# Adaptive max pooling: one 1 MB run of the input per partition, 47.5 KB loads pooled by one instruction each, two stores

## The chip, the cores and the metric

The kernel runs on one core of a Trainium2 chip; nothing else runs on the chip. The metric is the device time of an execution in microseconds (us), medians of several runs. All runs quoted here are with a granted clock of 1.0. KB and MB in sizes of runs and pitches are powers of two (1 MB = 1,048,576 bytes); MB and GB/s in the lines of the profile are decimal.

## The reference

The input is 32 x 256 x 4096 fp32 (134.2 MB), the output 32 x 256 x 256 fp32 (8.4 MB). The length is a multiple of the output size, so every window has 16 elements and none overlap:

```python
for i in range(output_size):
    start = int(i * length / output_size)
    end = int((i + 1) * length / output_size)
    result[:, :, i] = np.max(x[:, :, start:end], axis=-1)
```

In memory this is a maximum over each 16 consecutive numbers of a flat array. How the array is dealt out to the 128 partitions is free, and that is what the change is about.

## The kernel before

There are 8192 rows of 16 KB. 63 x 128 of them are cut into three regions; in each region a partition owns 21 consecutive rows. A load takes three rows (48 KB) per partition into a ring of nine row slots, three instructions on VectorE pool them, and all stores are issued after the last load. The last 128 rows are a load and a store of their own.

```python
    RING = 9
    G = 21
    N_GROUPS = 3
    LOAD = 3
    CUT = 15
    ...
    xg = xf[0:main].rearrange("(g p r) (o w) -> g p r o w", p=P, r=G, w=W)
    og = of[0:main].rearrange("(g p r) m -> g p (r m)", p=P, r=G)
    ...
    for g in range(N_GROUPS):
        for r in range(0, G, LOAD):
            at = n_read % RING
            nc.sync.dma_start(
                out=ring[:, at : at + LOAD], in_=xg[g][:, r : r + LOAD]
            )
            for i in range(LOAD):
                pooled(outs[g][:, (r + i) * O : (r + i + 1) * O], ring[:, at + i])
            n_read += LOAD
    ...
    for g in range(N_GROUPS - 1):
        nc.sync.dma_start(out=og[g], in_=outs[g])
    for a, b in ((0, CUT), (CUT, G)):
        ...
    nc.scalar.dma_start(out=ol, in_=spare)
```

Neighbouring partitions start 21 x 16 KB = 336 KB apart in HBM. This distance is called the pitch below.

Of the kernel before, what the change touches and what calls it, by code (L numbers as in the profile page):

```python
# [1 line left out]

# [4 lines left out]


@with_exitstack
def kernel(  # L10
    ctx: ExitStack,
    tc: tile.TileContext,
    x: bass.AP,
    output_size: bass.AP,
    out: bass.AP,
):



    nc = tc.nc  # L20
    P = nc.NUM_PARTITIONS
    fp32 = mybir.dt.float32

    B, C, L = x.shape
    O = int(output_size)
    assert L % O == 0, (L, O)
    W = L // O
    xf = x.flatten_outer_dims()
    of = out.flatten_outer_dims()
    rows = xf.shape[0]  # L30
    assert rows == 64 * P

    RING = 9
    G = 21
    N_GROUPS = 3
    LOAD = 3
    CUT = 15

    pool = ctx.enter_context(tc.tile_pool(name="pool", bufs=1))
    ring = pool.tile([P, RING, O, W], fp32, tag="ring", name="ring")  # L40
    outs = [
        pool.tile([P, G * O], fp32, tag=f"out{i}", name=f"out{i}")
        for i in range(N_GROUPS)
    ]

    main = N_GROUPS * G * P
    xg = xf[0:main].rearrange("(g p r) (o w) -> g p r o w", p=P, r=G, w=W)
    og = of[0:main].rearrange("(g p r) m -> g p (r m)", p=P, r=G)
    xl = xf[main:rows].rearrange("p (o w) -> p o w", w=W)
    ol = of[main:rows]  # L50

    def pooled(dst, src):
        nc.vector.reduce_max(out=dst, in_=src, axis=mybir.AxisListType.X)  # L53

    n_read = 0
    for g in range(N_GROUPS):
        for r in range(0, G, LOAD):
            at = n_read % RING
            nc.sync.dma_start(  # L59
                out=ring[:, at : at + LOAD], in_=xg[g][:, r : r + LOAD]  # L60
            )
            for i in range(LOAD):
                pooled(outs[g][:, (r + i) * O : (r + i + 1) * O], ring[:, at + i])
            n_read += LOAD

    at = n_read % RING
    spare = ring[:, (at + LOAD) % RING].rearrange("p o w -> p (o w)")[:, 0:O]
    nc.sync.dma_start(out=ring[:, at], in_=xl)
    pooled(spare, ring[:, at])

    for g in range(N_GROUPS - 1):
        nc.sync.dma_start(out=og[g], in_=outs[g])
    for a, b in ((0, CUT), (CUT, G)):
        nc.sync.dma_start(
            out=og[N_GROUPS - 1][:, a * O : b * O],
            in_=outs[N_GROUPS - 1][:, a * O : b * O],
        )
    nc.scalar.dma_start(out=ol, in_=spare)


# [1 line left out]
_INS = ['x', 'output_size']  # L82
_OUTS = [((32, 256, 256), 'float32')]

_NUMBERS = {'output_size': 256}


# [26 lines left out]
```

## Time and profile before

| | before |
|---|---|
| time, median of 6 runs | 335.94 us (335.76 to 336.12) |
| span of the profiled run | 334.3 us |
| moved by DMA | 142.6 MB, 427 GB/s over the span |
| queue of the loads and stores, share of the 16 engines' span | 98.9% |
| VectorE busy | 278.8 us (83%) |
| spacing of two loads of 6.29 MB | 14.53 us |

These lines are from the page of the kernel before: busy time by engine, bandwidth in 40 equal slices of the span, and the main DMA queue (packets, MB, share).

```profile
span 334.3 us, 157 instructions
...
DVE 278.8 (83%) x64; POOL 0.2 (0%) x4
...
GB/s 371 382 465 453 400 465 394 453 459 394 465 394 453 459 394 465 394 453 459 394 465 394 453 459 394 465 394 448 459 400 459 400 447 459 400 459 388 437 426 297
...
q1 hardware_dynamic: 3744, 142.48, 98.9%
...
```

The queue is full nearly from end to end, with 98.9% of the 16 engines' span: the transfers are the limit. The next lines, from the timeline of the same run, say the same of VectorE: start, duration, what ran, and in brackets how long VectorE had been idle and what it waited for.

```profile
...
start us, us, engine line op out<-in xcount [idle before <-releaser]
...
18.44 13.07 DVE L53 TENSOR_REDUCE out<-ring 128x256 f32<-128x4096 f32 x3 [18.44 <-DMA ring<-in_x_dram]
32.94 13.07 DVE L53 TENSOR_REDUCE out<-ring 128x256 f32<-128x4096 f32 x3 [1.43 <-DMA ring<-in_x_dram]
47.48 13.07 DVE L53 TENSOR_REDUCE out<-ring 128x256 f32<-128x4096 f32 x3 [1.47 <-DMA ring<-in_x_dram]
62.01 13.07 DVE L53 TENSOR_REDUCE out<-ring 128x256 f32<-128x4096 f32 x3 [1.45 <-DMA ring<-in_x_dram]
...
```

Each group of three reductions takes 13.07 us and the next load lands 14.53 us after the last (32.94 - 18.44 is 14.50, 47.48 - 32.94 is 14.54), so VectorE idles 1.46 us per load. 6.29 MB in 14.53 us is 433 GB/s. The windows view gives the bandwidth in stretches of the run (window, its length, VectorE busy and count, POOL busy and count, clock, DMA share, GB/s). The first stretch is the start-up, which matters below.

```profile
...
core 0: us, DVE busy (x) POOL busy (x), PEclk, DMA share, GB/s
5.00:35.00 30.00, 15.13 (x4) 0.00 (x0) 1.00 0.98 426
40.00:160.00 120.00, 108.31 (x26) 0.00 (x0) 1.00 1.00 433
...
```

The packet records of the trace are very even (a packet is one entry of these records; the 21 loads of 48 KB runs left 2688 of 48 KB, one per partition and load). A packet of 48 KB most often takes 1815 ns, one of 21 KB 799 ns. These two fit bytes / 27.2 GB/s plus about 9 ns per packet; this is called the fit below (packets of 15 and 6 KB took 573 and 234 ns, where it gives 574 and 235, and packets of 4 bytes 9 ns). 128 such packets per load or store are eight for each of the 16 engines in the mean.

### The profile page before, as it was taken

To read this page: it belongs to the slowest core of one execution; us is meant where nothing else is said; L and a number is where in the kernel's file an instruction comes from. 1 tells how busy PE (TensorE), PEld (TensorE's weight loads), DVE (VectorE), ACT (ScalarE), POOL (GpSimd) and SP (SyncE) were. 2 spreads that over 40 slices of the span, in tenths; PEclk is the share of its full clock that TensorE was granted. 3 is DMA by queue.
4 is the path that set the end of the run, shared out by engine and by line. 5 is a ranking of instruction groups with operands and counts; after the bars stand their busy time and mean duration, and the time that the engine had idled before them with its cause. 6 is when DMAs were issued, how large, how long until landed. Compare 5 with 4: busy or idle time off the path is not lost.

```text
span 334.3 us, 157 instructions
## 1 busy us (share of the span) xinstructions
DVE 278.8 (83%) x64; POOL 0.2 (0%) x4
## 2 busy tenths in 40 slices
DVE  0078989898898989889898898989889898988990
POOL 0000000000000000000000000000000000000000
DMA  9899999999999999999999999999999999999997
GB/s 371 382 465 453 400 465 394 453 459 394 465 394 453 459 394 465 394 453 459 394 465 394 453 459 394 465 394 448 459 400 459 400 447 459 400 459 388 437 426 297
DMA packets 3889, 142.62 MB, mean 427 GB/s; under 512 B 432, under 2 KB 560, under 8 KB 688
## 3 DMA queue, kind: packets, MB, share of 16 engines
q1 hardware_dynamic: 3744, 142.48, 98.9%
q10 hardware_dynamic: 144, 0.13, 0.1%
q14 instruction: 1, 0.01, 0.0%
HBM read 134.22 MB, written 8.39 MB: 427 GB/s over the span
## 4 chain that ended last, share of the span: by engine, by line
DMA 68%; DVE 26%; DVEq 2%; SPq 0%; issue 0%
DMA ring<-in_x_dram 68%; DVE out L53 25%; DVEq L109 2%; DVE ring L53 1%; SPq L59 0%
## 5 line engine op out<-in xcount | busy, mean ns | idle before, releaser
L53 DVE TENSOR_REDUCE out<-ring 128x256 f32<-128x4096 f32 x63 | 274.5, 4412 | 47.6 <-DMA ring<-in_x_dram 47.6
L53 DVE TENSOR_REDUCE ring<-ring 128x256 f32<-128x4096 f32 x1 | 4.4, 4410 | 0.0
L95 POOL MEMSET const-bfloat16-1.0<- 128x1 bf16 x1 | 0.1, 101 | 0.0
L95 POOL MEMSET const-uint8-127<- 128x1 uint8 x1 | 0.1, 101 | 0.0
L95 POOL MEMSET const-float32-0.0<- 128x1 f32 x1 | 0.1, 98 | 0.2 <-issue 0.2
L95 POOL MEMSET const-float32-1.0<- 128x1 f32 x1 | 0.1, 98 | 0.0
## 6 DMA issues: line engine op xcount, KB each, us to landing
ring<-in_x_dram SPq DMA_DIRECT2D x21, 6144.0 KB, 30.5
out_dram<-out SPq DMA_DIRECT2D x2, 2688.0 KB, 38.4
ring<-in_x_dram SPq DMA_DIRECT2D x1, 2048.0 KB, 29.5
out_dram<-out SPq DMA_DIRECT2D x1, 1920.0 KB, 38.2
out_dram<-out SPq DMA_DIRECT2D x1, 768.0 KB, 11.2
out_dram<-ring ACTq DMA_DIRECT2D x1, 128.0 KB, 6.4
```

The source lines that it names most:

```text
L53: nc.vector.reduce_max(out=dst, in_=src, axis=mybir.AxisListType.X)
L95: nc = _bacc.Bacc("TRN2", target_bir_lowering=False, num_devices=1)
L109: with _tile.TileContext(nc) as tc:
```

## The change

The intent is larger and fewer pieces: a partition owns one run of 1 MB of the flat input, a load takes 47.5 KB of it (three slots and all 64 KB of outputs make 206.5 KB per partition; the kernel before takes 207 KB), one reduction of 12160 elements pools it instead of three of 4096, and the outputs leave in two stores of 59 and 5 KB per partition instead of five stores. The diff, cut to its core:

```diff
-    RING = 9
-    G = 21
-    N_GROUPS = 3
-    LOAD = 3
-    CUT = 15
+    SLOTS = 3
+    CHUNK = 760
+    GROUPS = [total]
+    CUT = 20 * CHUNK
...
-    ring = pool.tile([P, RING, O, W], fp32, tag="ring", name="ring")
+    ring = pool.tile([P, SLOTS, CHUNK * W], fp32, tag="ring", name="ring")
...
+    for g, n in enumerate(GROUPS):
+        xg = xw[first : first + P * n].rearrange("(p n) w -> p (n w)", p=P)
+        og = ow[first : first + P * n].rearrange("(p n) -> p n", p=P)
+        first += P * n
+        for a in range(0, n, CHUNK):
+            b = min(a + CHUNK, n)
+            slot = ring[:, n_loads % SLOTS, 0 : (b - a) * W]
+            n_loads += 1
+            nc.sync.dma_start(out=slot, in_=xg[:, a * W : b * W])
+            nc.vector.reduce_max(
+                out=outs[g][:, a:b],
+                in_=slot.rearrange("p (n w) -> p n w", w=W),
+                axis=mybir.AxisListType.X,
+            )
+        if g < len(GROUPS) - 1:
+            stores.append((og, outs[g]))
+        else:
+            for a, b in ((0, CUT), (CUT, n)):
+                stores.append((og[:, a:b], outs[g][:, a:b]))
...
+    for dst, src in stores:
+        nc.sync.dma_start(out=dst, in_=src)
```

It also moves the pitch, from 336 KB to exactly 1 MB.

More of the change, by code (lines that the diff above doesn't have):

```diff
@@ L27 @@
     W = L // O
-    xf = x.flatten_outer_dims()
-    of = out.flatten_outer_dims()
-    rows = xf.shape[0]
-    assert rows == 64 * P
-    RING = 9
-    G = 21
-    N_GROUPS = 3
-    LOAD = 3
-    CUT = 15
+    total = B * C * O // P
+    SLOTS = 3
+    CHUNK = 760
+    GROUPS = [total]
+    CUT = 20 * CHUNK
+    assert sum(GROUPS) == total and B * C * O % P == 0
     pool = ctx.enter_context(tc.tile_pool(name="pool", bufs=1))
-    ring = pool.tile([P, RING, O, W], fp32, tag="ring", name="ring")
+    ring = pool.tile([P, SLOTS, CHUNK * W], fp32, tag="ring", name="ring")
@@ L41 @@
     outs = [
-        pool.tile([P, G * O], fp32, tag=f"out{i}", name=f"out{i}")
-        for i in range(N_GROUPS)
-    ]
-    main = N_GROUPS * G * P
-    xg = xf[0:main].rearrange("(g p r) (o w) -> g p r o w", p=P, r=G, w=W)
-    og = of[0:main].rearrange("(g p r) m -> g p (r m)", p=P, r=G)
-    xl = xf[main:rows].rearrange("p (o w) -> p o w", w=W)
-    ol = of[main:rows]
-    def pooled(dst, src):
-        nc.vector.reduce_max(out=dst, in_=src, axis=mybir.AxisListType.X)
-    n_read = 0
-    for g in range(N_GROUPS):
-        for r in range(0, G, LOAD):
-            at = n_read % RING
-            nc.sync.dma_start(
-                out=ring[:, at : at + LOAD], in_=xg[g][:, r : r + LOAD]
-            )
-            for i in range(LOAD):
-                pooled(outs[g][:, (r + i) * O : (r + i + 1) * O], ring[:, at + i])
-            n_read += LOAD
@@ L66 @@
-    at = n_read % RING
-    spare = ring[:, (at + LOAD) % RING].rearrange("p o w -> p (o w)")[:, 0:O]
-    nc.sync.dma_start(out=ring[:, at], in_=xl)
-    pooled(spare, ring[:, at])
-    for g in range(N_GROUPS - 1):
-        nc.sync.dma_start(out=og[g], in_=outs[g])
-    for a, b in ((0, CUT), (CUT, G)):
-        nc.sync.dma_start(
-            out=og[N_GROUPS - 1][:, a * O : b * O],
-            in_=outs[N_GROUPS - 1][:, a * O : b * O],
-        )
-    nc.scalar.dma_start(out=ol, in_=spare)
+        pool.tile([P, n], fp32, tag=f"out{i}", name=f"out{i}")
@@ new lines @@
+        for i, n in enumerate(GROUPS)
+    ]
+    xw = x.flatten_outer_dims().rearrange("r (o w) -> (r o) w", w=W)
+    ow = out.flatten_outer_dims().rearrange("r o -> (r o)")
+    stores = []
+    n_loads = 0
+    first = 0
+    for g, n in enumerate(GROUPS):
[11 more added lines that the diff above has]
+                axis=mybir.AxisListType.X,
+            )
+        if g < len(GROUPS) - 1:
[3 more added lines that the diff above has]
+                stores.append((og[:, a:b], outs[g][:, a:b]))
```

## The prediction

> **What bounds it now.** The DMA engines. The page's DMA row is 9 tenths in nearly every slice; queue q1 takes 98.9% of the 16 engines' span. The chain of waits alternates a load (30.5 us) with three reductions (13.1 us) because a ring slot must come free, but VectorE is not the limit: the timeline shows a 6.29 MB load pooled in 13.07 us and the next landing 14.53 us after it (1.46 us idle each time), so loads run at 433 GB/s. The packet records are even: a 48 KB packet takes a median of 1815 ns (5 to 95%: 1815 to 1824), a 21 KB one 799 ns, which fits bytes / 27.2 GB/s + 9 ns. Eight packets per engine and transfer: 21 x 8 x 1815 + 8 x 611 + 8 x (2 x 799 + 573 + 234) + 8 x 46 ns = 329.4 us of a 334.3 us span. About 5 us are start and last landing.
>
> **What changes.** Bytes stay (134.2 MB in, 8.4 MB out). By that fit a 47.5 KB packet takes 1796 ns, the last load's 26.5 KB 1006 ns, the stores' 59.4 KB 2243 ns and 4.6 KB 183 ns: 21 x 14.37 + 8.05 + 17.94 + 1.46 = 329.2 us. Larger runs save 0.2 us. VectorE goes from 64 instructions to 22; 4409 ns for 4096 elements, 4357 ns from start to start, means about 12.8 us for 12160 elements, still under 14.37 us, so none of this is critical. A slot comes free some 14 us before its load's turn. The last reduction ends near 326 us; the long store keeps the queue busy to about 330, so the short one joins in time. The last small store from the ACT queue disappears. If packets keep their rate: 334.5 to 336.5 us, nothing gained.
>
> **The risk.** Partitions were 336 KB apart (21 rows of 16 KB); now they are 1 MB apart, so all 16 engines read, in step, addresses congruent modulo 1 MB. [...] Nothing in this trace shows it. [...] I hold loss and no loss about equally likely; a gain over 2% is nearly excluded, since 329 us of packets remain.
>
> **Time.** The cases are about 335.5 us and 345 to 390 us; I record 340 us, 80% range 333 to 390. Faster by over 2%: 0.03; within 2%: 0.50; slower: 0.47.
>
> **What would show it.** No loss: load spacing in the timeline about 14.4 us, packets near 1796 ns, VectorE idle about 1.5 us before each reduction, bandwidth about 427 GB/s. Loss: spacing 15 to 17 us, packets over 1850 ns and uneven, idle over 2.5 us per reduction, bandwidth below 415, while the stores (64 KB pitch) stay near 430. Two stores at the end, no gap in the queue.
>
> **What would make it wrong.** [...]slow 59 KB store packets; a gap between the last reduction and the short store.

The recorded sum is 340 us, set between about 335.5 us without a loss and 345 to 390 us with one. "Nothing in this trace shows it" speaks of that loss. "In step" is, in the records of the kernel before, 1.3 us between the 16 engines at the end of each load.

## The result

The changed kernel takes 340.83 us (median of 6 runs, 340.21 to 341.89) against 335.94 us. The ratio is 1.0151, 95% interval 1.0131 to 1.0171: slower by 1.5%, clear of noise, within the 2% that count as the same. A ratio here is the mean time of one kernel's fast runs over that of the other's of the same rounds, so it is not quite the ratio of the medians quoted beside it.

| | before | changed |
|---|---|---|
| span of the profiled run | 334.3 us | 339.3 us |
| bandwidth over the span | 427 GB/s | 420 GB/s |
| bandwidth from 5 to 35 us | 426 GB/s | 391 GB/s |
| bandwidth from 40 to 160 us | 433 GB/s | 432 GB/s |
| first load pooled from | 18.44 us | 20.40 us |
| VectorE busy | 278.8 us | 276.3 us |

The page of the changed kernel, the same lines as before:

```profile
span 339.3 us, 110 instructions
...
DVE 276.3 (81%) x22; POOL 0.2 (0%) x4
...
GB/s 275 413 396 384 424 442 447 407 442 436 430 424 442 447 396 442 447 424 430 442 447 413 430 447 436 413 442 447 413 436 442 436 413 442 447 419 414 458 416 215
...
q1 hardware_dynamic: 3456, 142.61, 98.5%
...
```

The bytes are the same (the old kernel's last store, 0.13 MB, ran on another queue, q10); the bandwidth is low in the first slices (275, 413, 396, 384 where it was 371, 382, 465, 453). The timeline shows the landings one by one:

```profile
...
20.40 12.82 DVE L59 TENSOR_REDUCE out<-ring 128x760 f32<-128x12160 f32 x1 [20.40 <-DMA ring<-in_x_dram]
36.07 12.82 DVE L59 TENSOR_REDUCE out<-ring 128x760 f32<-128x12160 f32 x1 [2.85 <-DMA ring<-in_x_dram]
50.66 12.82 DVE L59 TENSOR_REDUCE out<-ring 128x760 f32<-128x12160 f32 x1 [1.77 <-DMA ring<-in_x_dram]
65.18 12.82 DVE L59 TENSOR_REDUCE out<-ring 128x760 f32<-128x12160 f32 x1 [1.71 <-DMA ring<-in_x_dram]
79.89 12.82 DVE L59 TENSOR_REDUCE out<-ring 128x760 f32<-128x12160 f32 x1 [1.88 <-DMA ring<-in_x_dram]
94.24 12.82 DVE L59 TENSOR_REDUCE out<-ring 128x760 f32<-128x12160 f32 x1 [1.53 <-DMA ring<-in_x_dram]
...
```

The first load lands 1.96 us later than before although it is a little smaller. The second follows after 15.67 us (36.07 - 20.40), the next after 14.59, 14.52 and 14.71. Then the spacing is 14.35 to 14.39 us, except for one more of 14.71. A load of 6.23 MB in 14.38 us is 433 GB/s, full rate. The windows agree:

```profile
...
5.00:35.00 30.00, 12.82 (x1) 0.00 (x0) 1.00 0.99 391
40.00:160.00 120.00, 106.56 (x9) 0.00 (x0) 1.00 1.00 432
...
```

So about two thirds of the 5 us arise in the first two loads: 2.1 us at the first landing (1.96, and 0.15 because this load is smaller), 1.3 at the second (15.67 against 14.38). Another 1.0 us lies in the three other long gaps and the one at load 8 (counted from 0, as below). That is 4.4 us up to the last full load. Most of the rest lies in the end: the 26.5 KB packets of the last load took 1059 ns in the mean where the fit gives 1006, 0.4 us for eight.

The packet records show the same from below. In the mean over the engines, the eight packets of load 0 took 2.2 us more than the fit and those of load 1 another 1.5 us; before, it was 0.6 and 0.0 us. (The single slowest packet tells nothing: 3.2 us in both kernels, in load 0.) Over the whole run the median is 1796 ns, exactly the fit, and the 95th percentile is 1960 ns, where the kernel before has 1824 for its slightly larger packets. The 59 KB packets of the large store took 2244 ns, again the fit. The records also say how far apart the 16 engines are: each load leaves 16 packets of 4 bytes, read here as one at the end of each engine's share, and from the first of these to the last it is 1.7 us at load 0 of the changed kernel, 2.6 at load 4 and 2.8 to 2.9 from load 8 to load 20 (some expectations below speak of about 2 us). The distance grows at each long gap (1.7, 1.8, 2.1, 2.2 and 2.6 us at loads 0 to 4, then 2.9 at load 8). In the kernel before it is 1.3 us in every load.

### The profile page after: what moved, and what is told of

It reads as the page before. It is cut to its first block, busy times and chain, and to the rows that moved or that the text cites. A ratio compares the mean times of both kernels' runs of the same rounds, so it can differ in the third digit from the quotient of the medians.

```text
span 339.3 us, 110 instructions
## 1 busy us (share of the span) xinstructions
DVE 276.3 (81%) x22; POOL 0.2 (0%) x4
## 3 DMA queue, kind: packets, MB, share of 16 engines
q1 hardware_dynamic: 3456, 142.61, 98.5%
## 4 chain that ended last, share of the span: by engine, by line
DMA 68%; DVE 26%; DVEq 2%; SPq 0%; issue 0%
DMA ring<-in_x_dram 68%; DVE out L59 26%; DVEq L102 2%; SPq L58 0%
## 5 line engine op out<-in xcount | busy, mean ns | idle before, releaser
L59 DVE TENSOR_REDUCE out<-ring 128x760 f32<-128x12160 f32 (+1 forms) x22 | 276.3, 12565 | 53.9 <-DMA ring<-in_x_dram 53.9
```

Source lines behind the costliest of these rows:

```text
L59: nc.vector.reduce_max(out=outs[g][:, a:b], in_=slot.rearrange("p (n w) -> p n w", w=W), axis=mybir.AxisListType.X,)
```

## The experiments

Three explanations were open. L: at a pitch of 1 MB, engines that start together read addresses that are congruent modulo a large power of two and get in each other's way until they have drifted apart. T: the first touch of a region spread over 128 MB is dear, whatever the exact pitch. S: the new sizes of packets and stores. Twelve runs were made; in the four with a wrong pitch the outputs are wrong and only the time counts. In the groups of runs below the kernel before took 335.96 to 336.05 us, so their times can be compared.

### The changed kernel again

> The changed kernel again, unaltered, as a control on this chip. Every theory: 340 to 342 us, ratio to before 1.013 to 1.017; reductions 0, 1 and 2 start near 20.4, 36.1 and 50.7 us, later ones 14.4 us apart.

No edit. Measured: 340.90 us, ratio 1.0142 (1.0126 to 1.0157). The result repeats.

### The pitch alone, put into the kernel before

```diff
-    xg = xf[0:main].rearrange("(g p r) (o w) -> g p r o w", p=P, r=G, w=W)
-    og = of[0:main].rearrange("(g p r) m -> g p (r m)", p=P, r=G)
-    xl = xf[main:rows].rearrange("p (o w) -> p o w", w=W)
-    ol = of[main:rows]
+    xp = xf.rearrange("(p r) (o w) -> p r o w", p=P, w=W)
+    op = of.rearrange("(p r) m -> p (r m)", p=P)
+    xg = [xp[:, g * G : (g + 1) * G] for g in range(N_GROUPS)]
+    og = [op[:, g * G * O : (g + 1) * G * O] for g in range(N_GROUPS)]
+    xl, ol = xp[:, 63], op[:, 63 * O :]
```

> The kernel before with its addresses alone changed: partition p owns rows 64p to 64p+63 (1 MB apart) instead of 21 rows in each of three regions (336 KB apart). Loads, packets, reductions and stores keep their sizes. Theory L (engines that start together read addresses congruent modulo 1 MB and collide until they have drifted apart): ratio about 1.010 to 1.017, first load landing near 20.4 us, second gap 15.5 to 16 us, then 14.53 us. Theory T (what is dear is the first touch of a region spread over 128 MB, whatever the exact pitch): the same, 1.010 to 1.017. Theory S (the changed sizes of packets and stores): 1.000.

Measured: 340.46 us, ratio 1.0127 (1.0113 to 1.0141). The instructions and the sizes of packets and stores are those of the old kernel, and the addresses alone bring nearly the whole loss (4.5 us over the kernel before, where the changed kernel has 4.9). Its timeline:

```profile
...
19.72 13.07 DVE L55 TENSOR_REDUCE out<-ring 128x256 f32<-128x4096 f32 x3 [19.72 <-DMA ring<-in_x_dram]
35.10 13.07 DVE L55 TENSOR_REDUCE out<-ring 128x256 f32<-128x4096 f32 x3 [2.30 <-DMA ring<-in_x_dram]
49.79 13.07 DVE L55 TENSOR_REDUCE out<-ring 128x256 f32<-128x4096 f32 x3 [1.62 <-DMA ring<-in_x_dram]
...
```

First landing at 19.72 us instead of 18.44, second gap 15.38 us instead of 14.53. This rules out S as the main cause.

### The pitch alone, taken out of the changed kernel

```diff
-    GROUPS = [total]
+    GROUPS = [21 * CHUNK, total - 21 * CHUNK]
...
-        if g < len(GROUPS) - 1:
+        if g > 0:
```

The 21 full chunks of a partition now form one run of 997.5 KB, and the last 26.5 KB come from a second region at the end of the input. The loads have the same sizes as in the changed kernel; the small store becomes two.

> The changed kernel with the pitch alone taken away: two groups, 21 chunks of 47.5 KB at a pitch of 997.5 KB and the last chunk of 26.5 KB at its own pitch; packets of the loads as in the changed kernel. Theory L: 335.5 to 336.5 us (ratio 0.998 to 1.002), first landing near 18.3 us, gaps 14.37 us from the second load on. Theory T (first touch of a region spread over 128 MB): unchanged from the changed kernel, about 341 us, since the first load touches the same span. Theory S (sizes of packets and stores): about 341 us.

Measured: 335.74 us (335.45 to 335.97), ratio to before 0.9990 (0.9978 to 1.0003). The loss is gone, 5.2 us against the changed kernel on the same chip (340.90 - 335.74). The timeline and the windows of this run:

```profile
...
17.94 12.82 DVE L59 TENSOR_REDUCE out<-ring 128x760 f32<-128x12160 f32 x1 [17.94 <-DMA ring<-in_x_dram]
32.30 12.82 DVE L59 TENSOR_REDUCE out<-ring 128x760 f32<-128x12160 f32 x1 [1.54 <-DMA ring<-in_x_dram]
46.69 12.82 DVE L59 TENSOR_REDUCE out<-ring 128x760 f32<-128x12160 f32 x1 [1.57 <-DMA ring<-in_x_dram]
...
```

```profile
...
5.00:35.00 30.00, 15.52 (x2) 0.00 (x0) 1.00 1.01 436
40.00:160.00 120.00, 107.50 (x9) 0.00 (x0) 1.00 1.01 435
...
```

The first landing is at 17.94 us, the spacing 14.36 us from the second load on, and the first 30 us run at 436 GB/s. The first load touches nearly the same 128 MB as in the changed kernel, so T is ruled out too. This is also the best version found, but it is not clear of the kernel before: the interval contains 1.

### How far from 1 MB is far enough

Three runs keep every size of the changed kernel and shorten the pitch of the loads alone (wrong outputs), by 4 KB, 1 KB and 256 bytes; a fourth halves it, so that its loads touch only about half of the input, most of it twice. The stores keep their pitch of 64 KB in all four. The 0.04 us for 1 KB is worked out from the fit (1024 bytes / 27.2 GB/s); which engines 1 KB would separate was not shown.

```diff
+    PITCH = (2**20 - 4096) // 4      # also - 1024, - 256, and 2**19
...
-            nc.sync.dma_start(out=slot, in_=xg[:, a * W : b * W])
+            at = min(a * W, P * n * W - P * PITCH)
+            xa = flat[at : at + P * PITCH].rearrange("(p k) -> p k", p=P)
+            nc.sync.dma_start(
+                out=slot, in_=xa[:, a * W - at : b * W - at]
+            )
```

> Wrong result on purpose: the changed kernel, each partition's run starting 4 KB less than 1 MB after the one before[...]. All sizes as in the changed kernel. Theory L: the collisions are nearly gone, 335.5 to 337 us. Theory T and theory S: about 341 us.

> Wrong result on purpose: a pitch 1 KB short of 1 MB[...], between 256 bytes short (77% of the cost left) and 4 KB short (none left). [...]Where it takes a distance that adds up to the 2 us of spread seen in the settled engines[...]: a quarter or less of the 5 us is left, 336 to 337.3 us. Neither tells those two apart; over 338.5 us refutes both.

> Wrong result on purpose: a pitch 256 bytes short of 1 MB[...]. Theory L[...]: still about 340 to 341 us. Theory L[...]: 335.5 to 336.5 us. A separation of 1 KB is 0.04 us of an engine's time at 27 GB/s[...].

> Wrong result on purpose: a pitch of 512 KB, all else as in the changed kernel. Theory L with full congruence at any large power of two: about 340 to 341 us. [...]

| pitch | time | over the 335.74 us at 997.5 KB |
|---|---|---|
| 1 MB | 340.90 us | 5.2 us |
| 1 MB - 256 bytes | 339.83 us | 4.1 us |
| 1 MB - 1 KB | 335.89 us | 0.2 us |
| 1 MB - 4 KB | 335.90 us | 0.2 us |
| 512 KB | 336.15 us | 0.4 us |

1 KB less was enough (0.2 us left) and 256 bytes less was not (4.1 us left); the differences of 0.2 us are within the spread of the runs. Since the stores kept their pitch, the loss lies in the loads. Of the expectations, L was right for 4 KB and, within 0.2 us, for 1 KB; 256 bytes left most of the cost, 339.83 us, near the higher of the two times that L gave. In the run with 256 bytes the first load lands earlier than in the changed kernel, but the first gap is even longer (34.91 - 18.72 is 16.19 us):

```profile
...
18.72 12.82 DVE L65 TENSOR_REDUCE out<-ring 128x760 f32<-128x12160 f32 x1 [18.72 <-DMA ring<-in_x_dram]
34.91 12.82 DVE L65 TENSOR_REDUCE out<-ring 128x760 f32<-128x12160 f32 x1 [3.36 <-DMA ring<-in_x_dram]
...
```

At 512 KB, one gap is left (14.93 us), and it is short. Of the two expectations, the one that full congruence at any large power of two costs as much as 1 MB (340 to 341 us) was wrong:

```profile
...
18.03 12.82 DVE L65 TENSOR_REDUCE out<-ring 128x760 f32<-128x12160 f32 x1 [18.03 <-DMA ring<-in_x_dram]
32.96 12.82 DVE L65 TENSOR_REDUCE out<-ring 128x760 f32<-128x12160 f32 x1 [2.11 <-DMA ring<-in_x_dram]
47.35 12.82 DVE L65 TENSOR_REDUCE out<-ring 128x760 f32<-128x12160 f32 x1 [1.56 <-DMA ring<-in_x_dram]
...
```

So a pitch that is a large power of two is not enough for the loss of 1 MB: 512 KB left 0.4 us of it. Why was not shown; the records here do not say which engine read which partition.

### Does the cost come back after a stop?

Load 11 is given the slot of load 10, so that it must wait until load 10 is pooled; the same in the kernel at 997.5 KB.

```diff
-            slot = ring[:, n_loads % SLOTS, 0 : (b - a) * W]
+            s = n_loads if n_loads < 11 else n_loads - 1
+            slot = ring[:, s % SLOTS, 0 : (b - a) * W]
```

> The changed kernel with one forced stop in the middle: load 11 reuses the slot of load 10, so it can only be issued once load 10 is pooled, and loads 11 to 13 then start on idle engines, as at the launch. Theory L (engines that start together collide): the cost comes a second time. Reduction 11 follows the restart about 2 us later than in the twin at 997.5 KB and the gap to reduction 12 is about 1 us longer than there; the twin is 6 to 11 us faster in all. Theory C (only the first microseconds of a launch, or the first touch of these addresses, are dear): no second cost; the twin is about 5 us faster, as without the stop.

> The same forced stop in the kernel with a pitch of 997.5 KB. Theory L and theory C: the stop costs one reduction and one fresh start, some 15 to 18 us, and no gap between reductions after it is longer than 14.5 us.

Measured: 348.23 us at 1 MB and 338.11 us at 997.5 KB. The expected length of the stop was wrong: the scheduler of the framework issued load 12, whose slot was free, ahead of load 11. So instead of one stop of some 15 us there were two short ones, where load 11 waited for the pooling of load 10, and where load 14, the next in that slot, waited for that of load 11. They were worth 2.4 us at 997.5 KB (338.11 - 335.74). At 1 MB the same stops cost 7.3 us (348.23 - 340.90). The timelines, first at 1 MB, then at 997.5 KB:

```profile
...
180.95 12.82 DVE L60 TENSOR_REDUCE out<-ring 128x760 f32<-128x12160 f32 x1 [1.54 <-DMA ring<-in_x_dram]
198.62 12.82 DVE L60 TENSOR_REDUCE out<-ring 128x760 f32<-128x12160 f32 x1 [4.86 <-DMA ring<-in_x_dram]
213.41 12.82 DVE L60 TENSOR_REDUCE out<-ring 128x760 f32<-128x12160 f32 x1 [1.96 <-DMA ring<-in_x_dram]
231.66 12.82 DVE L60 TENSOR_REDUCE out<-ring 128x760 f32<-128x12160 f32 x1 [5.43 <-DMA ring<-in_x_dram]
246.03 12.82 DVE L60 TENSOR_REDUCE out<-ring 128x760 f32<-128x12160 f32 x1 [1.55 <-DMA ring<-in_x_dram]
...
```

```profile
...
176.15 12.82 DVE L60 TENSOR_REDUCE out<-ring 128x760 f32<-128x12160 f32 x1 [1.56 <-DMA ring<-in_x_dram]
191.96 12.82 DVE L60 TENSOR_REDUCE out<-ring 128x760 f32<-128x12160 f32 x1 [3.00 <-DMA ring<-in_x_dram]
206.34 12.82 DVE L60 TENSOR_REDUCE out<-ring 128x760 f32<-128x12160 f32 x1 [1.56 <-DMA ring<-in_x_dram]
221.58 12.82 DVE L60 TENSOR_REDUCE out<-ring 128x760 f32<-128x12160 f32 x1 [2.42 <-DMA ring<-in_x_dram]
235.96 12.82 DVE L60 TENSOR_REDUCE out<-ring 128x760 f32<-128x12160 f32 x1 [1.56 <-DMA ring<-in_x_dram]
...
```

At 997.5 KB, the idle times after the two stops are 3.00 and 2.42 us, at 1 MB 4.86 and 5.43 us, with 1.96 us also in between. The windows around the stops, in the same order:

```profile
...
180.00:240.00 60.00, 46.80 (x4) 0.00 (x0) 1.00 0.96 392
240.00:300.00 60.00, 53.76 (x5) 0.00 (x0) 1.00 1.01 434
...
```

```profile
...
180.00:240.00 60.00, 51.47 (x5) 0.00 (x0) 1.00 0.99 424
240.00:300.00 60.00, 53.75 (x5) 0.00 (x0) 1.00 1.01 435
...
```

The stretch with the stops runs at 392 GB/s at 1 MB and at 424 at 997.5 KB; after it, both are at full rate. The twins differ by 10.1 us with the stops and by 5.2 without, within the 6 to 11 us that L gave, but not all of the 4.9 us between (7.3 - 2.4) is the cost of collisions come back. The packet records of the two profiled runs split it. The packets of the four loads from the first stop on took 3.3 us per engine more than the fit at 1 MB and 1.5 us at 997.5 KB: about 1.8 us is slower packets, against some 3 us in the first two loads of a launch. At the two stops together the engines stood idle for 4.6 us in the mean at 1 MB and 1.3 us at 997.5 KB: about 3.3 us is longer idling. That fits the distance of the engines before the first stop, 3.6 us at 1 MB and 0.9 us at 997.5 KB: a load is pooled only after its last engine is done (in the changed kernel, 0.3 to 0.5 us after the last 4-byte packet of the load), the restart waits for that pooling, and so the early engines wait longer. So the cost is not one of the launch or of first touching the data alone; a smaller part of it came back when the queue had run dry and the engines started again.

### Shorter runs

Two runs use loads of 16 KB per partition instead of 47.5 KB.

```diff
-    SLOTS = 3
-    CHUNK = 760
+    SLOTS = 8
+    CHUNK = 256
...
-    CUT = 20 * CHUNK
+    CUT = 59 * CHUNK
```

> The changed kernel with loads of 16 KB runs (64 loads of 2 MB, 8 slots) at the pitch of 1 MB[...]. If the loss at 1 MB is only the engines drifting apart once (about 2 us of spread, whatever the packet): 5 us over the twin at 1008 KB and full spacing (about 4.9 us a load) after the first 10 loads. If short runs keep the streams colliding (theory R): a loss in every load[...].

> The twin of the 16 KB runs at a pitch of 1008 KB. By the packet fit (614 ns for 16 KB against 1796 for 47.5 KB) 0.4 us of extra packet cost in all: 336 to 337 us, every load spaced by about 4.9 us.

Measured: 340.08 us at 1 MB and 339.30 us at 1008 KB. Two things came out differently than expected. First, 16 KB runs cost 3.6 us even at the harmless pitch (339.30 - 335.74), where I had written 0.4: 64 loads instead of 22 give each engine 42 x 8 = 336 more packets, and at 9 ns each that is 3.0 us. I had the rate per packet right and multiplied wrongly. Second, the two pitches differ by only 0.8 us, where one theory said 5 us and the other a loss in every load. The profiled run at 1 MB, the fastest of its four (339.80 to 340.81 us), shows no start-up loss at all (the twin has its first landing at 8.93 us and the next 4.88 us later); most of the 0.8 us is one late gap of 5.54 us:

```profile
...
8.88 4.42 DVE L59 TENSOR_REDUCE out<-ring 128x256 f32<-128x4096 f32 x1 [8.88 <-DMA ring<-in_x_dram]
13.71 4.42 DVE L59 TENSOR_REDUCE out<-ring 128x256 f32<-128x4096 f32 x1 [0.41 <-DMA ring<-in_x_dram]
...
224.24 4.42 DVE L59 TENSOR_REDUCE out<-ring 128x256 f32<-128x4096 f32 x1 [0.47 <-DMA ring<-in_x_dram]
229.78 4.42 DVE L59 TENSOR_REDUCE out<-ring 128x256 f32<-128x4096 f32 x1 [1.12 <-DMA ring<-in_x_dram]
...
```

Until that gap its engines were only 1.1 to 1.2 us apart at the end of a load. That looked as if short runs were immune. The last run tests this: the changed kernel, with the first 48 KB of each partition loaded as three loads of 16 KB runs.

```diff
-        for a in range(0, n, CHUNK):
-            b = min(a + CHUNK, n)
+        edges = [0, 256, 512] + list(range(768, n, CHUNK)) + [n]
+        for a, b in zip(edges, edges[1:]):
```

> The changed kernel at its pitch of 1 MB, with the first 48 KB of every partition loaded as three loads of 16 KB runs; then 20 loads of 47.5 KB runs and a rest of 26 KB. Theory A (the cost belongs to the first 30 us after a start, and 16 KB runs do not pay it): 335.5 to 336.8 us, long loads spaced 14.4 us from the first. Theory B (the cost belongs to long runs while the engines are less than about 2 us apart; short runs collide little, so they do not drive the engines apart): the first two long loads pay as the changed kernel's do, gaps of 15 to 17 us, 339 to 341 us in all.

Measured: 339.86 us, ratio 1.0121 (1.0104 to 1.0138). The timeline:

```profile
...
9.77 4.42 DVE L59 TENSOR_REDUCE out<-ring 128x256 f32<-128x4096 f32 x1 [9.77 <-DMA ring<-in_x_dram]
15.39 4.42 DVE L59 TENSOR_REDUCE out<-ring 128x256 f32<-128x4096 f32 x1 [1.20 <-DMA ring<-in_x_dram]
20.40 4.42 DVE L59 TENSOR_REDUCE out<-ring 128x256 f32<-128x4096 f32 x1 [0.59 <-DMA ring<-in_x_dram]
35.64 12.82 DVE L59 TENSOR_REDUCE out<-ring 128x760 f32<-128x12160 f32 x1 [10.82 <-DMA ring<-in_x_dram]
49.98 12.82 DVE L59 TENSOR_REDUCE out<-ring 128x760 f32<-128x12160 f32 x1 [1.53 <-DMA ring<-in_x_dram]
...
```

The short loads do pay here: the first lands at 9.77 us instead of 8.88, the second 5.62 us later instead of 4.83, and the first long load then comes 15.24 us after the last short one (35.64 - 20.40) instead of 14.4. After that the spacing is 14.3 to 14.4 us, but for two gaps of 14.59 and 14.52 us near 122 and 137 us. Neither theory was right: A said that short runs do not pay, B that the first two long loads pay as before. These first three loads read the same addresses in the same packets as the kernel of 64 short loads. What differs is what is queued behind them and how the engines happened to start: with eight slots, eight loads had been issued there by 4.9 us; with three slots, nothing was issued here behind the three until the pooling of the first freed its slot at 14.2 us. What decides whether short runs collide is therefore open.

## Why the prediction was right, and where it was not

- **What bounds the kernel.** Right. The DMA queue had 98.5% of the span after the change, and VectorE waited for loads alone.
- **Sizes and instruction counts gain nothing.** Right. The fit gave 1796 ns and 2243 ns for the new packets; the medians are 1796 and 2244. The reduction takes 12.82 us (12.8 predicted) and ends before the next load lands. With the pitch taken out, everything else in the change is worth 0.2 us (335.97 - 335.74 on the same chip), inside the noise.
- **The stores.** Right: full rate at their pitch of 64 KB (2244 ns for a packet of 59 KB, where the fit gives 2243).
- **The pitch as the risk.** Right in kind. What was measured is 391 GB/s from 5 to 35 us, 10% under the 436 GB/s at 997.5 KB; 16 KB loads at 1 MB lost only 0.8 us in all.
- **How long the loss lasts.** Here a step failed: I took the loss as a rate and applied it to the whole 310 us of load time. Most of it was over after about 30 us; it was some 5 us in all, where the recorded case with a loss lay 9.5 to 54.5 us over the one without (345 to 390 us against 335.5).
- **The number.** 340 us was the balance between two cases, 335.5 and 345 to 390 us, and neither happened. That the measured 340.83 us is close to it is luck: a third case lay in between. The signs that I gave for loss and no loss came mixed: one gap of 15.67 us, then 14.5 to 14.7 and at last 14.4; a bandwidth of 420 GB/s, between the 415 and the 427 that were to tell.

What is shown: the pitch alone is the cause, in both directions (the kernel before at 1 MB, the changed kernel at 997.5 KB and at 1 KB less than 1 MB), and most of the cost belongs to starts: some 3 us at the launch, about 1.8 us after the two later stops together. What is only argued: that the engines recover because they have drifted apart. In the changed kernel they are 2.8 to 2.9 us apart once they have settled, and the distance grew with each long gap, which fits. But no run set that distance by itself, and one speaks against it as a general rule: with 16 KB runs at 1 MB, engines 1.1 to 1.2 us apart lost next to nothing for some 220 us. What it is that collides was not shown; no run here looks inside HBM. Also open are the single late gaps, such as the one at load 8, and the slower packets of the last load, that of 26.5 KB.

## What to carry to other kernels

When a tensor is dealt out to partitions, look at the pitch in HBM that the layout makes, and try another where it is a large power of two: here exactly 1 MB cost 5.2 us and 512 KB 0.4 us, and splitting off a small tail region so that the pitch became 997.5 KB brought back all of the loss. The cost of a pitch need not be a lower rate throughout (here 391 GB/s from 5 to 35 us and 432 from 40 to 160 us); look at the spacing of the first few loads and at the loads after every stall, since the mean over the span hides it. After a stall, separate slower packets from idle engines before calling it a collision (here about 1.8 us and 3.3 us). In a stream that fills the DMA queue, count packets before hoping for a gain from larger ones: here 48 KB packets left 9 of 1815 ns to gain, and 16 KB packets cost 1% more.
